# Low rotary keys on 128 partitions, and the probability scale on ScalarE, in a two-layer diffusion backbone

## The chip, the cores and the metric

One core of a Trainium2 chip runs the whole program. The metric is the device time of one launch in microseconds (us). Five engines work side by side, each through its own instructions in order: TensorE (PE; its weight loads are listed apart as PEld), VectorE (DVE), ScalarE (ACT), GpSimd (POOL) and SyncE (SP), which here issues DMAs. The granted TensorE clock is given as a share of 2.4 GHz.

## The reference, cut to what matters

Layer 0 is latent attention (8 heads, 512 latent queries against 256 context and 512 latent keys) and a squared-ReLU MLP; layer 1 is a gated MLP and another squared-ReLU MLP. The change touches the attention of layer 0 alone. There a key has 128 plain dimensions of its own head and 64 rotary dimensions that all heads share (`k_pe`), normed together:

```python
k_pe = jnp.broadcast_to(k_pe[:, :, None, :], (B, S, MLA_HEADS, QK_ROPE))
k = rmsnorm(jnp.concatenate([k_nope, k_pe], axis=-1), k_norm)
...
s = jnp.einsum('bqhd,bkhd->bhqk', qi, k, preferred_element_type=jnp.float32) * scale
p = jax.nn.softmax(s, axis=-1)
return jnp.einsum('bhqk,bkhd->bqhd', p.astype(v.dtype), v)
```

## The kernel before

Every fp32 operand of a matmul is split into a high part, rounded to the matmul's format, and a low part, the rest, and a product is the sum of high·high, high·low and low·high (`mm3`, lines 79 to 82). ACT makes the high part with a cast, DVE the low part by a subtraction (`split`, lines 70 to 77).

Attention (lines 604 to 717) goes through 16 steps, a head and a half of its queries each. The loop at line 703 writes down `scores` of the next step, then `values` of this one, and then filler work: projections of the next heads' keys, values and queries (`kv_proj`, `q_proj`), the output projection of finished heads (`out_proj`), and background steps that sum up the modulation weights on DVE (`ada_steps`, line 165). The last step's output projection is `out_last`. The order in which the engines get the instructions is not this one: a planner with a time model of its own (`schedule_with_timeline_sim`, line 982) sorts them by priority and expected readiness. The order on each engine is then fixed, and semaphores keep what depends apart.

`scores` (line 622) works on tiles of 128 queries by 768 keys, 32 of them in all. A tile takes ten matmuls of 384 columns: five pairs of operands, each over two halves of the keys (lines 630 to 633). The first three pairs are the plain dimensions. For the rotary dimensions the 64 high parts of a query and its 64 low parts lie one above the other on 128 partitions (`sq`, made at lines 311 to 319), and the high parts of the keys lie there twice (`rh`, line 536), so one pass gives (high + low)·high. The fifth pair is high·low: it takes the first 64 partitions of `sq` and the low parts of the keys, `rl`, a tile of 64 partitions (lines 216 and 537). Both come from one transposition of `kpe`, which holds the rotary keys twice side by side (line 530).

Then the softmax of the tile: a DVE instruction moves the scores out of PSUM, scaled, and takes their maximum (L637), DVE negates it (L639), ACT takes the exponential in place and its sum (L640), DVE takes the reciprocal of the sum (L641) and multiplies the 768 columns by it (L642). `values` transposes the result on PE (L655), ACT and DVE split it into `th` and `tl` (L72 and L73, from line 658), and PE multiplies with the values (L80 to L82 with output `o`). The score tile has one buffer in PSUM (`PS`), the probabilities `p` five in SBUF, the transposed ones `pt` three in PSUM.

Of the kernel before, what the change touches and what calls it, by code (L numbers as in the profile page):

```python
# [9 lines left out]
F32 = mybir.dt.float32  # L10
F32R = mybir.dt.float32r
BF16 = mybir.dt.bfloat16
AF = mybir.ActivationFunctionType
ALU = mybir.AluOpType
AX = mybir.AxisListType

P = 128
# [4 lines left out]
TOK = CTX + SEQ  # L22
# [4 lines left out]
ROPE = 64  # L27
# [19 lines left out]
def hybrid_dit_kernel(  # L47
# [7 lines left out]
    PE, ACT, DVE, POOL = nc.tensor, nc.scalar, nc.vector, nc.gpsimd  # L55
    SBUF, PSUM = bass.MemoryType.SB, bass.MemoryType.PSUM

    def pool(stack, name, bufs=1, space=SBUF, side="left"):
        return stack.enter_context(tc.tile_pool(name=name, bufs=bufs, space=space, side=side, reuse_waits="tile"))
# [150 lines left out]
    ap_ = pool(att, "att")  # L210
# [2 lines left out]
    cq_h = ap_.tile([P, 3, SEQ], F32R, name="cq_h")  # L213
    cq_l = ap_.tile([P, 3, SEQ], F32R, name="cq_l")
    rh = ap_.tile([P, TOK], F32R, name="rh")
    rl = ap_.tile([ROPE, TOK], F32R, name="rl")
    epk = ap_.tile([P, NT], F32, name="epk")
    cosT = ap_.tile([P, NT, ROPE], F32, name="cosT")
    sinT = ap_.tile([P, NT, ROPE], F32, name="sinT")
# [112 lines left out]
    with ExitStack() as ini_stack:  # L332
# [7 lines left out]
        def pt(name):  # L340
            return ps.tile([P, 512], F32, tag="t", bufs=2, name=name)

        def pa(name):
            return ps.tile([P, 512], F32, tag="a", bufs=6, name=name)
# [60 lines left out]
        with ExitStack() as xstack:  # L405
# [12 lines left out]
            for k in range(0, KT, 2):  # L418
                o = pa(f"xct{k}")
# [4 lines left out]
            for k in range(KT):  # L424
                o = pa(f"xt{k}")
# [7 lines left out]
        for t in range(NT):  # L433
            o = rp[0][:, t * P:(t + 1) * P] if t < 2 else rp[1][:, (t - 2) * P:(t - 1) * P]
# [18 lines left out]
        for k in range(KT):  # L453
# [6 lines left out]
            for t in range(NT):  # L460
                a_h, a_l = (ch, cl) if t < 2 else (hh[k], hl[k])
                s = bass.ts(t if t < 2 else t - 2, P)
# [23 lines left out]
        for t in range(NT):  # L486
# [8 lines left out]
            o = pt(f"ckt{t}")  # L495
            for j in range(2):
                PE.transpose(o[:, j * P:(j + 1) * P], ck[:, j * P:(j + 1) * P], ident)
            for j in range(2):
                s = slice(t * P, (t + 1) * P)
# [12 lines left out]
        for t in range(NL):  # L512
            o = pa(f"qa{t}")
            for k in range(KT):
                s = bass.ts(t, P)
# [15 lines left out]
        for u in range(2):  # L531
            o = pt(f"krt{u}")
            for j in range(3):
                PE.transpose(o[:, j * P:(j + 1) * P], kpe[:, 3 * u + j, :, :].rearrange("p a r -> p (a r)"), ident)
            s = slice(u * 384, (u + 1) * 384)
            ACT.copy(out=rh[:, s], in_=o[:, :384])
            DVE.tensor_tensor(out=rl[:, s], in0=o[:ROPE, :384], in1=rh[:ROPE, s].bitcast(F32), op=ALU.subtract)

        drain(kv0)

# [63 lines left out]
    with hst as st_:  # L604
# [17 lines left out]
        def scores(h, half):  # L622
            kh, kl, rk = Ks[h]
            rk = rk.rearrange("p (a b) -> p a b", a=2)
            qh, ql, sq, rq_ = Qs[h // 2]
            i = h % 2
            for t in (2 * half, 2 * half + 1):
                s = slice(t * P, (t + 1) * P)
                S = ps.tile([P, 2, 512], F32, tag="s", bufs=PS, name=f"s{h}{t}")
                ops = [(qh[:, i, s], kh), (qh[:, i, s], kl), (ql[:, i, s], kh), (sq[i][:, s], rh), (sq[i][:ROPE, s], rl)]  # L630
                for m, (a, b) in enumerate(ops):
                    for n in range(2):
                        PE.matmul(S[:, n, :384], lhsT=a, rhs=b[:, n * 384:(n + 1) * 384], start=m == 0, stop=m == 4)  # L633
                sm = hq.tile([P, 4], F32, tag="sm", bufs=4, name=f"sm{h}{t}")
                rq = rq_[:, t, i, 2:3]
                e = hq.tile([P, 2, 384], F32, tag="p", bufs=5, name=f"p{h}{t}")
                DVE.tensor_tensor_reduce(out=e, in0=S[:, :, :384], in1=rk, op0=ALU.mult, op1=ALU.max, scale=rq,  # L637
                                         scalar=-3.0e38, accum_out=sm[:, 0:1])
                DVE.tensor_scalar(out=sm[:, 1:2], in0=sm[:, 0:1], scalar1=-1.0, scalar2=None, op0=ALU.mult)  # L639
                ACT.activation(out=e, in_=e, func=AF.Exp, bias=sm[:, 1:2], accum_out=sm[:, 2:3])  # L640
                DVE.reciprocal(out=sm[:, 3:4], in_=sm[:, 2:3])  # L641
                DVE.tensor_scalar(out=e, in0=e, scalar1=sm[:, 3:4], scalar2=None, op0=ALU.mult)  # L642
                Pr[h, t] = e.rearrange("p a b -> p (a b)")

        def values(h, half):
# [45 lines left out]
        drain(q_proj(0)); ada_step(8)  # L691
        steps = [(h, half) for h in range(HEADS) for half in range(2)]
        scores(0, 0)
        drain(kv_proj(1))
        fill = {}
# [7 lines left out]
        for i, (h, half) in enumerate(steps):  # L703
            if i + 1 < len(steps):
                scores(*steps[i + 1])
            values(h, half)
            ada_step(ADS[i])
            for g, n in fill.get((h, half), []):
                drain(g, n)
            if i == len(steps) - 2:  # L710
                out_last(3, 0)
# [117 lines left out]
    with ExitStack() as st_:  # L829
# [7 lines left out]
        for q in range(4):  # L837
            ws = [W(gm_w_in, 2 * k2, 2, HALF + q * 512, 512, f"gv{q}{k2}") for k2 in range(4)]
            for ts in ((0, 1), (2, 3)) if q == 0 else ((0, 1, 2, 3),):
                acc = {t: (pu if t < 2 else pd)(f"v{q}{t}") for t in ts}  # L840
                for k in range(KT):
                    wh, wl = ws[k // 2]
                    for t in ts:
                        s = slice(t * P, (t + 1) * P)
                        mm3(acc[t], hs[k][0][:, s], hs[k][1][:, s], wh[:, k % 2, :], wl[:, k % 2, :], k == 0, k == KT - 1)
                for t in ts:
# [8 lines left out]
                            in_=gm_bs.rearrange("g p -> (g p)").unsqueeze(0).to_broadcast([P, G * P]))  # L855
        for g4 in range(2):
            o = pt(f"wst{g4}")
# [6 lines left out]
            o = pt(f"rsw{g4}")  # L864
# [33 lines left out]
        for t in range(NL):  # L898
# [3 lines left out]
                              op0=ALU.subtract, op1=ALU.mult)  # L902
# [83 lines left out]
```

## Time and profile before

| | |
|---|---|
| median of 3 runs | 1401.54 us (1399.29 to 1401.88) |
| the profiled execution | 1399.21 us |
| its span, from the first to the last instruction | 1397.4 us |
| busy: PE, DVE, ACT, POOL | 1355.4, 856.0, 545.6, 88.7 us |
| chain that ended last | PE 85%, issue 7%, DVE 3%, DMA 2%, ACT 1%, POOL 1% |
| granted TensorE clock, mean | 0.99 |

The profile is one execution. A busy share is an average over stages, and a PE that counts as busy may still stream fewer columns than it could, because a matmul's end is modelled. So a stage is read by the starts of neighbouring matmuls and by what its waits name.

### The profile page before, as it was taken

How to read it: one execution, taken by the hardware profiler on the slowest of the kernel's cores; microseconds unless marked ns; L12 is line 12 of the kernel's file. 1: busy time of each engine (PE TensorE's matmuls, PEld its weight loads, DVE VectorE, ACT ScalarE, POOL GpSimd, SP SyncE). 2: the span in 40 equal slices, each digit the busy share in tenths (PEclk: the TensorE clock that was granted, in tenths of full speed). 3: DMA queues.
4: the chain of work that ended last, by engine and by line, in shares of the span. 5: the costliest groups of instructions: out<-in, count | busy, mean ns of one | idle time of the engine just before them, and what ended most of it. 6: DMA issues, size and time to landing. Idle time of an engine off the chain costs nothing.

```text
span 1397.4 us, 18421 instructions
## 1 busy us (share of the span) xinstructions
PE 1355.4 (97%) x7159; PEld 1149.3 (82%) x7159; DVE 856.0 (61%) x1423; ACT 545.6 (39%) x1046; POOL 88.7 (6%) x140
## 2 busy tenths in 40 slices
PE   6989899999899999999999999999999999999998
PEld 4878889888898888888898888888888888888888
DVE  5876787887899888543457356555575344343442
ACT  6556556564652231322335233222254133231331
POOL 2031111100011111000000010000000000000000
PEclk9998999999999999999999999999999999999999
DMA  9551221311478878333323332222223222333311
GB/s 286 169 171 35 80 89 41 114 46 39 132 224 277 280 249 272 98 103 99 97 69 102 102 111 86 90 92 91 76 61 121 91 91 91 94 103 93 104 46 61
DMA packets 126823, 163.23 MB, mean 117 GB/s; under 512 B 7467, under 2 KB 111488, under 8 KB 126736
## 3 DMA queue, kind: packets, MB, share of 16 engines
q1 hardware_dynamic: 114784, 119.50, 27.0%
q0 software_dynamic: 11808, 42.03, 9.5%
q8 instruction: 56, 0.92, 0.3%
q10 hardware_dynamic: 144, 0.52, 0.1%
q14 instruction: 31, 0.25, 0.1%
HBM read 159.94 MB, written 2.10 MB: 116 GB/s over the span
## 4 chain that ended last, share of the span: by engine, by line
PE 85%; issue 7%; DVE 3%; DMA 2%; ACT 1%; POOL 1%; SPq 0%; POOLq 0%; DVEq 0%; ACTq 0%
PE s L633 3%; PE v L80 2%; PE v L82 2%; PE v L81 2%; DMA adr<-in_ada_w_dram 2%; PE pt L655 1%; PE wo L80 1%; PE f1d2o L82 1%; PE f1d0o L80 1%; PE f1d0o L81 1%; PE f1d2o L81 1%; PE f1d2o L80 1%; PE f1d0o L82 1%; PE f0d1o L80 1%; PE f0d1o L81 1%
## 5 line engine op out<-in xcount | busy, mean ns | idle before, releaser
L165 DVE SCALAR_TENSOR_TENSOR acc<-adr,sil,acc 128x1024 f32<-128x1024 f32 x70 | 89.7, 1281 | 20.7 <-DMA adr<-in_ada_w_dram 20.0
L161 POOL DMA_DIRECT2D adr<-in_ada_w_dram x80 | 43.4, 542 | 220.9 <-DVE acc L165 122.6
L782 DVE TENSOR_TENSOR f1a<-f1a 128x512 f32<-128x512 f32 (+1 forms) x36 | 22.5, 629 | 39.8 <-ACT f1a L781 39.8
L637 DVE CUSTOM_DVE_ANT_0 p<-s,rk,rq 128x768 f32<-128x768 f32 x32 | 32.5, 1015 | 14.1 <-PE s L633 11.9
L73 DVE TENSOR_TENSOR tl<-pt,th 128x512 fp32r<-128x512 f32 x48 | 32.7, 687 | 11.6 <-ACT th L72 11.2
L72 ACT CAST f0uh<-f0a 128x512 fp32r<-128x512 f32 (+1 forms) x36 | 20.4, 572 | 48.5 <-DVE f0a L782 48.5
L72 ACT CAST th<-pt 128x512 fp32r<-128x512 f32 x48 | 27.9, 589 | 23.6 <-PE o L82 13.6
L640 ACT ACTIVATE p<-p,sm 128x768 f32<-128x768 f32 x32 | 30.1, 940 | 15.1 <-DVE sm L639 15.1
L126 POOL TENSOR_TENSOR nst<-nst,mhalf 128x2 f32<-128x2 f32 x6 | 5.1, 854 | 457.5 <-DVE nst L125 457.5
L73 DVE TENSOR_TENSOR f1ul<-f1a,f1uh 128x512 fp32r<-128x512 f32 (+1 forms) x36 | 22.6, 632 | 18.8 <-ACT f1uh L72 18.6
L782 DVE TENSOR_TENSOR f0a<-f0a 128x512 f32<-128x512 f32 (+1 forms) x36 | 22.5, 627 | 18.4 <-ACT f0a L781 18.4
L72 ACT CAST f1uh<-f1a 128x512 fp32r<-128x512 f32 (+1 forms) x36 | 20.4, 572 | 32.0 <-DVE f1a L782 32.0
L73 DVE TENSOR_TENSOR f0ul<-f0a,f0uh 128x512 fp32r<-128x512 f32 (+1 forms) x36 | 22.4, 627 | 11.7 <-ACT f0uh L72 11.7
L81 PE MATMUL o<-tl,vh 128*128 128x256 f32 x96 | 28.1, 292 | 1.0 <-DVE tl L73 0.9
L80 PE MATMUL o<-th,vh 128*128 128x256 f32 x96 | 28.6, 298 | 0.0
L600 DVE SCALAR_TENSOR_TENSOR xT<-wo,mod,xT 128x512 f32<-128x512 f32 (+1 forms) x40 | 25.1, 638 | 5.2 <-PE wo L82 4.9
L655 PE MATMUL pt<-ident,p 128*128 128x128 f32 x192 | 27.7, 274 | 0.0
L82 PE MATMUL o<-th,vl 128*128 128x256 f32 x96 | 27.1, 282 | 0.0
L655 PEld LDWEIGHTS pt<-ident,p 128*128 128x128 f32 x192 | 22.2, 141 | 1.8 <-issue 1.0
L892 DVE TENSOR_TENSOR gm<-gm,u 128x512 f32<-128x512 f32 x16 | 11.0, 689 | 20.6 <-ACT u L873 20.5
L81 PEld LDWEIGHTS o<-tl,vh 128*128 128x128 f32 x96 | 18.2, 190 | 2.4 <-DVE tl L73 1.7
L642 DVE TENSOR_SCALAR p<-p,sm 128x768 f32<-128x768 f32 x32 | 19.8, 618 | 0.6
(2637 smaller groups left out, 4651.6 us busy)
## 6 DMA issues: line engine op xcount, KB each, us to landing
adr<-in_ada_w_dram POOLq DMA_DIRECT2D x80, 512.0 KB, 4.8
xn<-in_x_dram SPq DMA_DIRECT2D x4, 512.0 KB, 7.2
out_dram<-of SPq DMA_DIRECT2D x8, 256.0 KB, 2.2
xn<-in_ctx_dram SPq DMA_DIRECT2D x2, 512.0 KB, 4.1
ada000r<-in_ada_w_dram SPq DMA_DIRECT2D x1, 512.0 KB
ada001r<-in_ada_w_dram SPq DMA_DIRECT2D x1, 512.0 KB
ada100r<-in_ada_w_dram SPq DMA_DIRECT2D x1, 512.0 KB, 11.3
ada101r<-in_ada_w_dram SPq DMA_DIRECT2D x1, 512.0 KB, 10.2
```

What stands on the lines that cost most here:

```text
L72: ACT.copy(out=hi, in_=src)
L73: eng.tensor_tensor(out=lo, in0=src, in1=hi.bitcast(F32), op=ALU.subtract)
L80: PE.matmul(o, lhsT=wh, rhs=mh, start=start, stop=False)
L81: PE.matmul(o, lhsT=wh, rhs=ml, start=False, stop=False)
L82: return PE.matmul(o, lhsT=wl, rhs=mh, start=False, stop=stop)
L161: nc.gpsimd.dma_start(out=r, in_=ada_w[l][k * P:(k + 1) * P, ch * D:(ch + 1) * D])
L165: DVE.scalar_tensor_tensor(out=acc, in0=r, scalar=sil[:, k, 0:1], in1=acc, op0=ALU.mult, op1=ALU.add)
L633: PE.matmul(S[:, n, :384], lhsT=a, rhs=b[:, n * 384:(n + 1) * 384], start=m == 0, stop=m == 4)
L637: DVE.tensor_tensor_reduce(out=e, in0=S[:, :, :384], in1=rk, op0=ALU.mult, op1=ALU.max, scale=rq, scalar=-3.0e38, accum_out=sm[:, 0:1])
L640: ACT.activation(out=e, in_=e, func=AF.Exp, bias=sm[:, 1:2], accum_out=sm[:, 2:3])
L655: PE.transpose(T[:, j, q * P:(q + 1) * P], Pr[h, 2 * half + q][:, (2 * jp + j) * P:(2 * jp + j + 1) * P], ident)
L782: DVE.tensor_tensor(out=f, in0=f, in1=f, op=ALU.mult)
```

## The change

`rl` gets 128 partitions in place of 64 and is filled on all of them (the transposition already holds the keys twice, so the lower half is the same numbers again). The fifth pair of matmuls then takes all 128 partitions of `sq`: it adds low·low, which was left out before, to high·low. The number of matmuls and their columns stay. And the multiplication by the reciprocal of the sum, a DVE instruction, becomes an ACT instruction that copies in place with a scale of one number per partition.

```diff
-    rl = ap_.tile([ROPE, TOK], F32R, name="rl")
+    rl = ap_.tile([P, TOK], F32R, name="rl")
...
-            DVE.tensor_tensor(out=rl[:, s], in0=o[:ROPE, :384], in1=rh[:ROPE, s].bitcast(F32), op=ALU.subtract)
+            DVE.tensor_tensor(out=rl[:, s], in0=o[:, :384], in1=rh[:, s].bitcast(F32), op=ALU.subtract)
...
-                ops = [(qh[:, i, s], kh), (qh[:, i, s], kl), (ql[:, i, s], kh), (sq[i][:, s], rh), (sq[i][:ROPE, s], rl)]
+                ops = [(qh[:, i, s], kh), (qh[:, i, s], kl), (ql[:, i, s], kh), (sq[i][:, s], rh), (sq[i][:, s], rl)]
...
-                DVE.tensor_scalar(out=e, in0=e, scalar1=sm[:, 3:4], scalar2=None, op0=ALU.mult)
+                ACT.activation(out=e, in_=e, func=AF.Copy, scale=sm[:, 3:4])
```

## Rows read from the trace of the kernel before

**Rows 1.** Busy time by stage: us, engines' busy time (instructions), clock, DMA

```profile
119.00:352.00 233.00, 228.86 (x1493) 204.65 (x1491) 183.11 (x424) 137.14 (x393) 25.99 (x28) 0.99 0.21 66
352.00:385.00 33.00, 28.33 (x201) 26.61 (x201) 30.08 (x67) 20.69 (x42) 3.51 (x5) 0.90 0.46 146
```

**Rows 2.** Who waited for whom on PE, 119 to 352 us: total, times, longest

```profile
PE rkb L276 <- POOL st L271: 1.9, 1, 1.9
PE s L633 <- ACT qh L72: 1.4, 1, 1.4
PE o L81 <- DVE tl L73: 0.9, 2, 0.7
```

**Rows 3.** The score matmuls' line, L633: durations in ns (min/median/max), shapes, idle

```profile
L633 PE MATMUL s<-rh,sq x64: 332/338/340, 124.5 to 347.6; 128*128 128x384 f32 x64
L633 PEld LDWEIGHTS s<-rl,sq x64: 182/184/187, 124.9 to 347.9; 64*128 64x128 f32 x64
L633 PE MATMUL s<-rl,sq x64: 327/385/441, 124.9 to 348.1; 64*128 64x384 f32 x64
...
  issue: 7.8, 32
```

**Rows 4.** Timeline of PE and PEld, one score tile: start, us, engine, line

```profile
186.80 0.51 PE L633 MATMUL s<-kh,ql 128*128 128x384 f32 x2
187.15 0.51 PE L633 MATMUL s<-rh,sq 128*128 128x384 f32 x2
187.59 0.61 PE L633 MATMUL s<-rl,sq 64*128 64x384 f32 x2
188.13 0.38 PE L80 MATMUL o<-th,vh 128*128 128x256 f32 x1
188.36 0.28 PE L81 MATMUL o<-tl,vh 128*128 128x256 f32 x1
188.47 0.28 PE L82 MATMUL o<-th,vl 128*128 128x256 f32 x1
...
186.98 0.36 PEld L633 LDWEIGHTS s<-rh,sq 128*128 128x128 f32 x2
187.59 0.29 PEld L633 LDWEIGHTS s<-rl,sq 64*128 64x128 f32 x2 [0.25 <-issue]
188.13 0.19 PEld L80 LDWEIGHTS o<-th,vh 128*128 128x128 f32 x1 [0.25 <-issue]
```

**Rows 5.** Timeline of PE and PEld where weights of 4 rows follow

```profile
28.87 0.28 PE L389 MATMUL ada_o<-ada101l,c 128*4 128x256 f32 x1
...
28.75 0.09 PEld L389 LDWEIGHTS ada_o<-ada101l,c 128*4 128x4 f32 x1
29.08 0.52 PEld L394 LDWEIGHTS ada_c<-sel,adrow 4*128 4x128 f32 x4 [0.24 <-issue]
```

**Rows 6.** Lines L642, L640, and of ACT by shape (busy us, mean ns)

```profile
L642 DVE TENSOR_SCALAR p<-p,sm x32: 606/619/622, 131.1 to 351.6; 128x768 f32<-128x768 f32 x32
L640 ACT ACTIVATE p<-p,sm x32: 923/939/961, 129.0 to 350.4; 128x768 f32<-128x768 f32 x32
L640 ACT ACTIVATION_READ_ACCUMULATOR p<-p,sm x32: 182/190/222, 129.8 to 351.2; 128x1 f32 x32
...
L75 ACT ACTIVATE kh<-kt,gqk 128x512 fp32r<-128x512 f32 x7 | 4.9, 703 | 0.6 <-PE kt L265 0.6
```

**Rows 7.** Timeline of DVE, ACT and PE, the tile with the longest softmax

```profile
282.65 0.16 DVE L641 RECIPROCAL sm<-sm 128x1 f32<-128x1 f32 x1
284.96 0.61 DVE L642 TENSOR_SCALAR p<-p,sm 128x768 f32<-128x768 f32 x1
...
279.77 0.21 ACT L640 ACTIVATION_READ_ACCUMULATOR p<-p,sm 128x1 f32 x1
280.62 0.59 ACT L72 CAST th<-pt 128x512 fp32r<-128x512 f32 x1 [0.35 <-PE o L82]
...
282.65 0.36 PE L80 MATMUL o<-th,vh 128*128 128x256 f32 x1
...
289.38 0.60 PE L655 MATMUL pt<-ident,p 128*128 128x128 f32 x4
```

**Rows 8.** Timeline of ACT, DVE, PEld and PE, the last tile

```profile
351.31 1.06 ACT L72 CAST th<-pt 128x512 fp32r<-128x512 f32 x2
351.64 0.62 DVE L642 TENSOR_SCALAR p<-p,sm 128x768 f32<-128x768 f32 x1
352.91 0.19 PEld L81 LDWEIGHTS o<-tl,vh 128*128 128x128 f32 x1 [0.31 <-DVE tl L73]
354.75 1.04 PE L655 MATMUL pt<-ident,p 128*128 128x128 f32 x8
```

**Rows 9.** Busy time in a stretch of attention at a lower clock (columns of rows 1)

```profile
258.00:260.60 2.60, 2.60 (x8) 2.10 (x7) 1.82 (x5) 0.81 (x4) 0.98 (x2) 0.51 0.17 30
```

## Prediction

> **What bounds the kernel now.** The page comes first: PE is busy 97% of the span and takes 85% of the chain that ended last, so the question in each stage is whether PE streams as fast as it can. The change sits in attention, so I cut the span by stages. Attention runs from 119 to 352 us: PE is busy for 228.9 of its 233 us, DVE for 183.1 (79%) and ACT for 137.1 (59%) [rows 1]. In the next stage, to 385 us, DVE is busy for 30.1 of 33 us and PE for 28.3 [rows 1]; there PE is no longer alone at the bound. The waits of PE in attention name only 4.2 us: one of 1.9 us for POOL, one of 1.4 us for ACT, two for DVE [rows 2]. So neither ACT nor DVE holds PE up in attention, and a gain there has to come out of PE's own stream.
>
> Busy hides what that stream loses. The score matmuls' line shows it: of ten matmuls of a tile, those with `rl` alone use 64 rows. Their median duration is 385 ns against 338 for the same columns on 128 rows, and before the 64-row loads the load unit stands for 7.8 us in 32 times, with no wait named: 0.24 us once per tile [rows 3]. The timeline of one tile shows both ends. Pairs of 384 columns follow each other at 0.35 us (186.80 to 187.15). The 64-row pair starts 0.44 us after the pair before it, the next matmul 0.54 us after that, and the one behind, after only 256 columns, 0.23 us later, where the next takes 0.11 [rows 4]. The loads explain it: a 128-row load runs while the matmul before it streams (186.98, ahead of the pair at 187.15), but the first 64-row load starts when the last 128-row matmul has nearly ended (187.15 + 0.51 = 187.66 against 187.59), and the first 128-row load after it again starts late, at 188.13. Both have 0.25 us of idle load unit in front [rows 4]. Another place with few rows looks alike: a 4-row load waits 0.24 us, until the 128-row matmul that began at 28.87 and took 0.28 has nearly ended (29.15 against 29.08) [rows 5]. So it goes with the change in the number of rows, not with `rl` or its data.
>
> **The change part by part.**
>
> *128 rows in the fifth pair.* The ten matmuls keep their columns; what goes is the two switches. In an even stream the matmul at 188.36 would come 0.35 + 0.35 + 0.12 = 0.82 us after 187.15; it came after 1.21 [rows 4]. The excess is 0.39 us, and 32 tiles make 12.5 us, all in PE's queue. The added low·low product costs nothing in columns: the 128-row pair beside it is the price, 0.35 us a pair [rows 4]. Bounds: if only the entry's idle (7.8 us in all [rows 3]) went and the return stayed, 7.8; if both go, 12.5. I take 12.5, since the pairs ahead of the fifth are of exactly the form that it takes on.
>
> The TensorE page of the Trainium skill (TensorE: Matmul & The Clock Gate, section on packing small matmuls) says that a weight load overlaps a running matmul only when their row groups differ. By that rule 128 rows everywhere would be the bad case. The trace disagrees: the `rh` loads run under matmuls on the same 128 rows, and the loads that wait are those whose rows differ [rows 4].
>
> *The fill of `rl`* is done on 128 partitions in place of 64, twice, before the scores begin: the columns are the same, as is the partition's share of SBUF. I cost it at nothing; the cover is that the same instruction already runs there.
>
> *The multiplication leaves DVE:* 32 × 0.619 = 19.8 us [rows 6], off an engine for which PE waits 0.9 us in this stage [rows 2]. On the path that is worth between 0 and that 0.9; I take 0.
>
> *The copy on ACT.* The trace has no copy of 768 columns with a scale per partition. The nearest rows are the exponential over the same 768 columns, SBUF to SBUF with a number per partition, at 0.939 us, and the scaled copy of 512 columns out of PSUM, at 0.703 [rows 6]. I take 0.94, from the same shape: 32 × 0.94 = 30.1 us. ACT's load in attention becomes (137.1 + 30.1) / (233 − 12.5) = 76%, DVE's (183.1 − 19.8) / 220.5 = 74%. Neither becomes the bound by its sum.
>
> The ScalarE page (ScalarE: Activation LUTs, rules for kernel authors) tells authors to keep multiplications on VectorE, not ScalarE. The durations agree with it, 0.62 us against about 0.94, but that is a matter of engine time, not of the path. Its formula for a pointer operand gives 0.92 us as an estimate.
>
> *The new wait.* The copy sits in ACT's queue and waits for the reciprocal, on DVE. Behind it on ACT queue the `th` casts, the `kn`, `vh` and `kh` evacuations and the next exponential; PE waits for the casts. If ACT reaches the copy at once after its exponential, it stands for the reciprocal (0.16 us) and two hand-overs, some 0.24 us as an estimate from the 0.16, and then works 0.94: 1.18 us for what is behind. In the tile with the longest softmax the sum was out at 279.98 (279.77 + 0.21), and the reciprocal came only at 282.65, behind other DVE work: an ACT queue stuck there would have lost 2.7 us. In that time ACT cast a `th` (280.62 to 281.21) that PE first read at 282.65, 1.4 us later [rows 7]. So a copy of 0.94 in front of a cast is covered in a typical place, 1.18 just so, 2.7 not. The planner decides which it is; since it knows the wait, I expect it to put the ready casts first, as it put them here before the scale.
>
> *The probabilities come later* by 0.94 − 0.62 = 0.32 us and by the queue. In the tight tile the scale ended at 285.57 and the transposition came at 289.38, 3.8 us later [rows 7]; in the last tile it ended at 352.26 and the transposition came at 354.75, 2.5 us later [rows 8]. Both cover it.
>
> *The tail.* At 351.31 ACT casts two `th`, and PE waits 0.31 us for their low halves [rows 8]. If the last copy is put ahead of those casts, PE loses the 1.18 us; if behind, nothing. I take half, 0.6.
>
> *Order and clock.* The planner gets other durations and may sort the stage anew. PE's clock was at 0.51, the level of 1.2 GHz, in the 2.6 us from 258.0, after single-column matmuls of the background; a stretch like it costs 1.3 us [rows 9]. One more or one fewer is ±1.3; I take 0.
>
> *Sum*, on the profiled execution (1399.2 us, its span 1397.4 and 1.8 around it): 1399.2 − 12.5 + 0.6 = 1387.3. After 352 us everything is released by what comes before it, so the gain is kept. The median of the runs lies 2.3 us above the profiled one; I put the forecast in the middle, 1388.5.
>
> **The rivals.**
>
> *ACT gets late and PE waits for it: slower.* The mechanism is the copy in front of `th` casts, with ACT standing for the reciprocal. The gain is gone when a tile costs PE over 0.39 us. For it speaks that PE leans on ACT at every `th`, 48 times, and that the copy can stand for up to 2.7 us [rows 7]; against it, that PE waited for ACT just once in 233 us [rows 2]. If half of the 1.18 us of each tile reaches PE, it costs 32 × 0.59 = 18.9 us: 1399.2 − 12.5 + 18.9 = 1405.6.
>
> *ACT takes back a part.* A quarter of the 1.18 us reaches PE: 32 × 0.3 = 9.4, so 1396.
>
> *The switch stays.* The change would not do what it says, if the idle belonged to `rl` as a second operand and not to its rows: 1399.2 to 1401.5. The 4-row loads speak against it [rows 5].
>
> *The page's rule on row groups holds.* Then each of the three loads at and after the fifth pair would wait for the matmul in front, at about 0.2 us each, 0.6 in place of 0.39: 32 × 0.2 = 6.4 us more, 1405.6. The running overlap at 186.98 speaks against it [rows 4].
>
> **How the numbers follow.** The forecast has 0.75; ACT taking back a part 0.12; the switch staying 0.05; ACT making it slower 0.07; the rule 0.01. A measurement of this kernel can tell about 0.2%, 2.8 us, from no change. So faster is 0.75 + 0.12 = 0.87, within 0.2% is 0.05, slower 0.08. The range: downward, the 4.2 us of waits [rows 2] and the clock's 1.3 us [rows 9] could go too: 1387.3 − 5.5 = 1381.8, so 1382. Upward it takes in the part taken back, 1396, with a little of the runs' spread: 1397.
>
> **What would show it.** In the profile after: 128-row loads for `rl` with no idle of 0.24 us before them and pairs at 0.35 us; a score matmul median of 338 ns in all five pairs; attention shorter by 12 us, to some 221; copies on ACT of about 0.94 us, 32 times; PE's waits for ACT in attention still a few us. I would be wrong if PE's waits for `th` and `tl` grow to over 10 us, if the 0.25 us stay before the `rl` loads, or if the next stage, to 385 us, grows by what attention gives.

## The result, and the profile after

| | before | after |
|---|---|---|
| median of 4 runs | 1401.71 us | 1390.88 us (1389.81 to 1392.8) |
| ratio, 95% interval | | 0.993 [0.9917, 0.9942] |
| the profiled execution, its span | 1399.21, 1397.4 us | 1390.98, 1389.2 us |
| busy: PE, DVE, ACT | 1355.4, 856.0, 545.6 us | 1346.8, 838.6, 569.6 us |

The kernel is faster by 0.7%, 10.8 us between the medians. The forecast was 1388.5 us; the measured time lies 2.4 us above it and inside the range.

The line of the score matmuls in the profile after, durations in ns (min/median/max), answers [rows 3]:

```profile
L633 PE MATMUL s<-kh,qh x64: 333/338/445, 121.0 to 342.3; 128*128 128x384 f32 x64
L633 PE MATMUL s<-rh,sq x64: 333/337/422, 126.0 to 343.4; 128*128 128x384 f32 x64
L633 PEld LDWEIGHTS s<-rl,sq x64: 187/188/193, 126.2 to 343.5; 128*128 128x128 f32 x64
L633 PE MATMUL s<-rl,sq x64: 334/338/423, 126.4 to 343.7; 128*128 128x384 f32 x64
...
  issue: 0.5, 1
```

The fifth pair now takes as long as the others, 338 ns in the median where it took 385, and of the 32 idle times of 7.8 us one of 0.5 is left. The timeline of PE and PEld in the tile that [rows 4] showed:

```profile
186.57 0.51 PE L633 MATMUL s<-kh,ql 128*128 128x384 f32 x2
186.92 0.51 PE L633 MATMUL s<-rh,sq 128*128 128x384 f32 x2
187.26 0.51 PE L633 MATMUL s<-rl,sq 128*128 128x384 f32 x2
187.61 0.60 PE L655 MATMUL pt<-ident,p 128*128 128x128 f32 x4
...
187.09 0.36 PEld L633 LDWEIGHTS s<-rl,sq 128*128 128x128 f32 x2
187.44 0.31 PEld L655 LDWEIGHTS pt<-ident,p 128*128 128x128 f32 x2
```

The pairs follow each other at 0.34 to 0.35 us through the fifth and into the next matmul, and the loads for `rl` (187.09) run while the `rh` pair (186.92 to 187.43) streams.

The stages, in the columns of [rows 1]; attention now ends earlier, so the first stretch takes in a few us of what follows:

```profile
119.00:352.00 233.00, 228.11 (x1561) 217.42 (x1560) 172.92 (x411) 166.88 (x436) 27.11 (x29) 0.99 0.21 66
```

In the same 233 us PE gets 1561 matmuls done in place of 1493. ACT is busy for 166.9 us in place of 137.1. The copies themselves, and what ACT waits for in front of them (the line of L642, durations in ns; then, from ACT's waits from 121 to 346.6 us, the one ahead of L642: total, times, longest):

```profile
L642 ACT ACTIVATE p<-p,sm x32: 929/942/1018, 131.4 to 346.7; 128x768 f32<-128x768 f32 x32
...
ACT p L642 <- DVE sm L641: 3.4, 6, 1.6
```

PE's waits in attention (121 to 354 us, columns of [rows 2], the three longest) stay small: 0.6 us for the low halves `tl`, far from the 10 us that the prediction named as a sign of being wrong.

```profile
PE q L80 <- DVE qg L304: 1.8, 1, 1.8
PE s L633 <- ACT qh L72: 0.8, 1, 0.8
PE o L81 <- DVE tl L73: 0.6, 2, 0.3
```

To see where the time went I take attention from the first score matmul's start (the `kh,qh` row of L633) to the last value matmul's start (the last of L82 with output `o`). Before, that is 119.5 to 361.6, 242.1 us; after, 121.0 to 353.8, 232.8 us: 9.3 us less, where the prediction's sign was 12. Up to the first score matmul the profiled execution of after lost 1.5 us, with the same instructions in the same order but for the shape of `rl`'s fill; among the runs below whose instructions are the same up to there, that start lies between 119.4 and 125.0 us. And `rl` itself is filled 1.3 us later already (107.9 us against 106.6), so the delay is older than the changed instruction and belongs to the execution. Behind attention the gain is kept: the last span differs by 8.2 us = 9.3 − 1.5 + 0.4.

### The profile page after: what moved, and what is told of

Its sections match the earlier page's. It is cut to its first block, busy times and chain, and to the rows that moved or that the text cites. A ratio compares the mean times of both kernels' runs of the same rounds, so it can differ in the third digit from the quotient of the medians.

```text
span 1389.2 us, 18418 instructions
## 1 busy us (share of the span) xinstructions
PE 1346.8 (97%) x7159; PEld 1153.9 (83%) x7159; DVE 838.6 (60%) x1391; ACT 569.6 (41%) x1078; POOL 89.1 (6%) x140
## 4 chain that ended last, share of the span: by engine, by line
PE 77%; issue 9%; DVE 6%; DMA 5%; ACT 2%; POOL 1%; SPq 0%; POOLq 0%; DVEq 0%; ACTq 0%
DMA adr<-in_ada_w_dram 5%; PE s L633 3%; PE v L82 2%; PE v L80 2%; PE v L81 2%; DVE acc L165 1%; PE pt L655 1%; PE f1d2o L80 1%; PE f1d0o L81 1%; PE f1d0o L82 1%; PE f1d0o L80 1%; PE f1d2o L81 1%; PE f1d2o L82 1%; PE f1d1o L80 1%; PE f0d2o L82 1%
## 5 line engine op out<-in xcount | busy, mean ns | idle before, releaser
L640 ACT ACTIVATE p<-p,sm 128x768 f32<-128x768 f32 x32 | 30.2, 943 | 12.6 <-DVE sm L639 12.5
L642 ACT ACTIVATE p<-p,sm 128x768 f32<-128x768 f32 x32 | 30.4, 950 | 3.4 <-DVE sm L641 3.4
L82 PE MATMUL o<-th,vl 128*128 128x256 f32 x96 | 27.1, 283 | 0.0
L633 PE MATMUL s<-kh,qh 128*128 128x384 f32 x64 | 18.3, 363 | 1.6 <-ACT qh L72 0.8
```

What stands on the lines that cost most here:

```text
L82: return PE.matmul(o, lhsT=wl, rhs=mh, start=False, stop=stop)
L642: ACT.activation(out=e, in_=e, func=AF.Copy, scale=sm[:, 3:4])
```

## The experiments

Theory A: the gain is the two changes of the row count in each score tile, and ScalarE's copy gives a small part back. The rivals are B (the copy is free; the planner's new order eats the rest), C (the freed VectorE is the gain), D (the cost goes with the 64-row matmuls, not with the change), and those that came up on the way.

The order of the instructions shows how clean each experiment is. With the rows alone, every engine has the order of before. With the copy alone, every engine has the order of after. So the four make a square: two orders, each with 64 and with 128 rows. The order comes with the copy, and the rows leave it alone.

In every table row, attention is measured as above. Beside it stands how long the granted clock was at 0.50, the level of 1.2 GHz, in that time, and from where on. In the profile after one such stretch lies at 163.4; its window (columns of [rows 1]):

```profile
163.40:166.80 3.40, 3.40 (x16) 3.40 (x16) 2.26 (x7) 1.32 (x5) 1.58 (x2) 0.50 0.57 165
```

Those come and go between executions of one kernel: the 128 rows alone had none in one profile and one in the next, and so had the whole change.

| kernel | ratio to before, 95% interval | attention, us | at half clock, us (from) |
|---|---|---|---|
| before | 1 | 242.1 | 3.4 (257.1) |
| after | 0.993 [0.9917, 0.9942] | 232.8 | 3.4 (163.4) |
| after, again | 0.9927 [0.9914, 0.9941] | 232.7 | 0 |
| 128 rows alone | 0.9922 [0.9901, 0.9942] | 230.4 | 0 |
| 128 rows alone, again | 0.9918 [0.9903, 0.9933] | 230.0 | 3.4 (165.5) |
| copy alone | 1.0006 [0.9992, 1.0019] | 245.9 | 6.8 (175.0, 260.3) |
| four changes of rows | 1.0083 [1.0061, 1.0106] | 253.2 | 0 |
| copy twice | 0.9986 [0.9974, 0.9999] | 238.8 | 10.2 (162.3, 176.0) |
| 96 rows | 0.9926 [0.9908, 0.9943] | 230.4 | 3.4 (161.5) |
| 72 rows | 0.992 [0.9901, 0.9938] | 231.1 | 3.4 (167.4) |
| 32 rows | 0.9999 [0.9986, 1.0011] | 240.6 | 0 |
| 128 rows, sums on VectorE | 0.9967 [0.9955, 0.998] | 228.5 | 0 |

What such a stretch costs can be read where two executions run the same matmuls in the same order. Those inside a stretch of 3.4 us take 1.5 to 1.6 us longer in every such pair. But part of it can come back. PE in the 128 rows alone, without a stretch and then with the one from 165.5 us:

```profile
169.84 0.51 PE L633 MATMUL s<-kl,qh 128*128 128x384 f32 x2
171.18 0.39 PE L81 MATMUL o<-tl,vh 128*128 128x256 f32 x1 [0.82 <-DVE tl L73]
```

```profile
174.87 0.51 PE L633 MATMUL s<-kl,qh 128*128 128x384 f32 x2
175.22 0.29 PE L81 MATMUL o<-tl,vh 128*128 128x256 f32 x1
```

The wait for `tl` that follows is gone in the second; I read that as the engines that feed PE drawing level while it was slow. So the two profiles differ by 0.4 us in attention (230.4 and 230.0), not by 1.6, and those of the whole change by 0.1 (232.7 and 232.8). The stretch of before, at 257.1, cost nearly all of its price: 32 rows, in the same order and without one, take 1.5 us less. So I compare profiles without a stretch where there are any. Where there are none I take off the price inside: 1.6 us for before (240.5) and, as an estimate that nothing came back, 3.1 for the copy alone (242.8).

### The rows alone

The change's three edits of `rl`; the scale stays `DVE.tensor_scalar`.

> The low rotary keys on 128 partitions alone; the scale by the reciprocal stays on VectorE. Theory A (the row switch was worth 0.39 us a tile, 12.5 us in all, and ScalarE's copy gave some 3 us of it back): ratio to the kernel before near 0.991, some 2 to 3 us faster than the whole change; the time from the first score matmul to the last value matmul falls from 242.1 us to about 230, and PE's excess over an even stream there, apart from the switches, stays at the 7.4 us of before. Rival B (the copy costs nothing, the gain is simply smaller because the planner sorted attention anew): the same ratio as the whole change, 0.993, and an excess of about 10 us here too.

Ratio 0.9922, attention 230.4 us. That is the gain of the whole change and, by the profiles, some 2 us more. Since PE's order is that of before, the two traces can be laid side by side, matmul by matmul: the steps at the fifth pair and right behind it are shorter by 11.5 us in all, 0.36 us a tile, and everything else by 0.2: the 1.6 us of half clock are gone, and 1.4 us came in as slightly longer steps elsewhere, 0.5 of it within the first pair of the score matmuls. What lengthens them the profile does not name. Theory A's sign holds. What it calls the excess did not stay: against an even stream, in which each matmul takes the median step of its number of columns (222.3 us in all), 8.1 us are left over here, and no half clock is in them as in the 7.4.

### The copy alone

The last edit of the change alone; `rl` and the fifth pair stay as before.

> The scale on ScalarE alone; the fifth pair of score matmuls keeps its 64 rows. Theory A: slower than before by 0 to 4 us (ratio 1.000 to 1.003), the 0.25 us of idle load unit ahead of the 64-row loads still there 32 times, and the excess over an even stream some 3 us up. Rival B: no change of time beyond 1 us in either direction, apart from what another order brings. Rival C (freed VectorE time is what gained, the rows nothing): 8 to 10 us faster.

Ratio 1.0006, with 1 inside the interval: moving VectorE's 19.8 us to ScalarE gains nothing, so rival C falls. (The same edit adds the copy to ScalarE, so it does not show what freeing VectorE would do by itself.) Attention is 245.9 us; without its two stretches at half clock some 242.8, against 240.5, so 2.3 us more. The waits of PE in attention, before in [rows 2], now:

```profile
PE o L81 <- DVE tl L73: 2.4, 3, 1.1
PE q L80 <- DVE qg L304: 1.8, 1, 1.8
PE s L633 <- ACT qh L72: 0.6, 1, 0.6
PE wo L80 <- DVE qg L304: 0.4, 1, 0.4
```

In all they name 5.2 us against 4.2. The wait for the low halves of the transposed probabilities, `tl`, went from 0.9 to 2.4 us. They are made from ACT's casts, which is the place that the prediction named for lateness.

### Four changes of the row count in place of two

```diff
-                for m, (a, b) in enumerate(ops):
-                    for n in range(2):
-                        PE.matmul(S[:, n, :384], ...)
+                for m, n in [(0, 0), (0, 1), (1, 0), (1, 1), (2, 0), (2, 1), (3, 0), (4, 0), (3, 1), (4, 1)]:
+                    a, b = ops[m]
+                    PE.matmul(S[:, n, :384], ...)
```

> The kernel before, with the last four score matmuls of a tile in the order 128 rows, 64 rows, 128 rows, 64 rows in place of two and two: the same ten matmuls, but four changes of the number of rows a tile in place of two. Theory A (the cost goes with the change of rows): slower by 32 x 0.39 = 12.5 us, ratio 1.009. Rival D (the cost goes with the 64-row matmuls or with the tile of the low keys, however they are ordered): no change, ratio 1.000.

Slower by 0.83% [0.61, 1.06], some 11.6 us; attention 253.2 us, 12.7 more than before without its half clock, where A said 12.5 and D nothing. The load unit's timeline in one tile:

```profile
192.06 0.19 PEld L633 LDWEIGHTS s<-rh,sq 128*128 128x128 f32 x1
192.50 0.18 PEld L633 LDWEIGHTS s<-rl,sq 64*128 64x128 f32 x1 [0.25 <-issue]
192.87 0.19 PEld L633 LDWEIGHTS s<-rh,sq 128*128 128x128 f32 x1 [0.18 <-issue]
193.24 0.18 PEld L633 LDWEIGHTS s<-rl,sq 64*128 64x128 f32 x1 [0.19 <-issue]
193.60 0.19 PEld L80 LDWEIGHTS o<-th,vh 128*128 128x128 f32 x1 [0.18 <-ACT p L640]
```

Each change of rows, in both directions, has its idle in front, and the loads that would run under a matmul in an even stream come 0.37 us apart where the matmuls need 0.17. The edit also puts two matmuls in a row on the same half of the score tile; that is not the cause, since the matmuls into `o` do the same at 0.11 us [rows 4]. The cost goes with the change; D falls.

### The copy twice

The whole change with `ACT.activation(out=e, in_=e, func=AF.Copy)` behind the first copy.

> The whole change with a second copy in place on ScalarE behind the first, so 30 us more on that engine (89% of attention) and 0.94 us more before the probabilities are ready. Theory A (PE pays for part of each copy through late casts, some 0.1 us each so far): the second costs more than the first, 5 to 15 us, ratio to before 0.997 to 1.004. Rival B (the copy lies beside PE's work and costs nothing): within 2 us of the whole change, ratio 0.993.

Ratio 0.9986, about 0.0058, 8 us, above the whole change. So the copies do not lie beside PE's work for nothing, and the second costs more than the first. In the profile attention is 238.8 us against 232.7 and 232.8, with 10.2 us at half clock against 0 and 3.4. The window from 160 to 200 us shows it, here and in the second profile of the whole change:

```profile
160.00:200.00 40.00, 36.25 (x223) 33.71 (x223) 31.31 (x71) 28.38 (x76) 7.90 (x11) 0.87 0.42 127
```

```profile
160.00:200.00 40.00, 35.30 (x236) 32.74 (x237) 31.86 (x73) 26.69 (x73) 8.92 (x11) 1.00 0.44 134
```

PE idles for about as long in both (3.8 and 4.7 us of 40), but the clock is at 0.87 in the first. One profile cannot say whether that is chance, but the runs say more: over the whole program the granted clock was 0.9868 in the mean of the 12 executions with two copies (0.984 to 0.989) and 0.9888 in that of the 10 of the whole change (0.987 to 0.991). That is 2.8 us of 1400, as an estimate, if PE loses all of it, so up to a third of the 8 us is clock. The waits that the profile names in attention sum to 6.7 us against 5.7 and 4.6; the rest has no name. PE's order is another here too, so the cost is that of the copy with its order.

### The rows and the whole change on one chip

> Once more the 128 rows alone, now on the same chip as the whole change. Theory A (ScalarE's copy costs PE little once the clock's dips, which come and go from one execution to the next, are set aside): ratio 0.992, attention 230 to 231 us from the first score matmul to the last value matmul without dips. It is 0.5 to 2 us faster than the whole change, less than the rounds can tell. Rival E (the copy costs some 3 us of the 12.5): 3 us faster than the whole change.

> The whole change again, on the same chip as the 128 rows alone. Theory A: ratio 0.992 to 0.994, attention 231 us after subtracting 1.7 us for each dip of the clock. Rival E: ratio 0.994 to 0.995.

0.9918 against 0.9927: 1.3 us, less than either interval. By the profiles without a stretch the whole change's attention is 232.7 us, that of the rows alone 230.4; by those with one it is 232.8 against 230.0, 230.4 and 231.1 (128, 96 and 72 rows, in the mean 230.5). So the copy costs PE 2.3 us in attention with 128 rows, and by the estimate above 2.3 with 64. By names, PE's waits in the second profile of the whole change sum to 5.7 us, in the first of the rows alone to 4.1 (1.9 + 1.4 + 0.8):

```profile
PE o L81 <- DVE tl L73: 1.9, 3, 0.9
PE q L80 <- DVE qg L304: 1.8, 1, 1.8
PE s L633 <- DVE sm L637: 0.6, 2, 0.4
PE s L633 <- ACT qh L72: 0.6, 1, 0.6
PE qrt L316 <- DVE qs L73: 0.4, 1, 0.4
PE wo L80 <- DVE qg L304: 0.4, 1, 0.4
```

That names 1.6 us of it, 1.1 for `tl`. Rival E's 3 us and A's 0.5 to 2 both lie within what the runs leave open; whether the copy or the order that comes with it is to blame cannot be told apart, since the planner makes the order from the copy.

### 96, 72 and 32 rows

From the rows alone, with `sq[i][:96, s]`, `sq[i][:72, s]` and `sq[i][:32, s]` in the fifth pair and `rl` cut alike. Every engine keeps its order.

> The 128-row version with the scale on VectorE, but the fifth pair of score matmuls takes 96 of its 128 rows (so a part of low times low is left out); every engine's order is that of the 128 rows alone. Theory A (any change of the number of rows costs the drain on both sides, 0.36 us a tile): slower than the 128 rows alone by 11.5 us, ratio to before near 1.000, 0.25 us of idle ahead of the 96-row loads. Rival F (the cost goes with the share of rows left out, or with half arrays alone): between 0.992 and 0.996.

> As the 96-row version, with 72 rows in the fifth pair of score matmuls. Theory G (what costs is a change between more than 64 rows and 64 or fewer; 72 rows count as a full array): like the 128 rows, ratio 0.992, no idle of 0.25 us ahead of the loads. Theory H (the cost depends on how far the rows fall below 128, and 96 was near enough): between 0.994 and 1.000.

> 32 rows in the fifth pair, so half of high times low is left out as well. Theory G: the same drain on both sides as with 64 rows, 11 to 12.5 us more than with 128 rows, ratio to before 0.999 to 1.001. Theory H: more than the 64 rows cost, ratio above 1.002. If only exactly half an array has the drain: 0.992.

With 96 rows theory A failed: ratio 0.9926, as with 128. Going from 128 rows to 96 and back costs nothing. That made theory G, that 64 rows or fewer are one case and more are another, and the last two runs bore it out: 72 rows 0.992, 32 rows 0.9999. Where between 64 and 72 the boundary lies, no run shows. The loads for `rl` in the three (busy us, mean ns, then the idle time before them):

```profile
L633 PEld LDWEIGHTS s<-rl,sq 96*128 96x128 f32 x64 | 11.6, 189 | 0.0
```

```profile
L633 PEld LDWEIGHTS s<-rl,sq 72*128 72x128 f32 x64 | 11.6, 189 | 0.0
```

```profile
L633 PEld LDWEIGHTS s<-rl,sq 32*128 32x128 f32 x64 | 9.4, 183 | 7.8 <-issue 7.8
```

With 32 rows the idle is 7.8 us in all, to the tenth what 64 rows had [rows 3], and attention takes 240.6 us against 240.5. The return to 128 rows costs the same idle again:

```profile
188.48 0.29 PEld L633 LDWEIGHTS s<-rl,sq 32*128 32x128 f32 x2 [0.25 <-issue]
189.02 0.19 PEld L80 LDWEIGHTS o<-th,vh 128*128 128x128 f32 x1 [0.25 <-issue]
```

So neither does the price grow as the rows get fewer: H falls too.

### The background sums on VectorE

The rows alone, and in `ada_steps` the three sums that fall in attention take the path of the later ones (`fast`): no single-column matmuls.

> The 128 rows alone, and the three background sums that fall in attention no longer use 48 single-column matmuls but the way of the later sums: a transposition and a reduction on VectorE and one matmul each. If PE's bursts of single-column matmuls cost their own time and bring the dips of the clock behind them: 3 x 1.7 us less on PE and up to 1.7 us for a dip that does not come, so 3 to 6 us faster than the 128 rows alone, ratio to before 0.988 to 0.990, and no dip between the first score matmul and the last value matmul. If VectorE's 3 x 2.5 us more, or the planner's other order, weigh as much: ratio 0.992 or above.

Ratio 0.9967, 7 us slower than the rows alone. The longest wait of PE in its profile stands ahead of attention, with two of the new DVE instructions shortly before its end (the line numbers are one higher in this kernel):

```profile
PE krt L535 <- DVE kpe L531: 7.6, 1, 7.6
...
102.47 1.23 DVE L174 STREAM_TRANSPOSE adr02t<-acc 128x1024 f32<-128x1024 f32 x1
105.71 1.21 DVE L175 TENSOR_REDUCE red<-adr02t 128x32 f32<-128x1024 f32 x1
```

The planner put the first sum among the rotation of the keys, for which PE waits, and the first score matmul came at 129.1 us. The two instructions are 2.4 of the 7.6 us; the rest goes with the other order. Attention then took 228.5 us with the single-column matmuls gone, 1.9 less than the rows alone without half clock (230.4). That is less than the 3 to 6 forecast, and less than what was lost ahead of it. No half clock appeared in attention, but neither did it in some kernels that kept the single-column matmuls, so this says nothing on what brings it.

## Why the prediction was right, and where not

**PE's stream bounds attention: right.** Moving 19.8 us from VectorE to ScalarE, where it takes 30.1, gained nothing and cost some 2 us by the profiles, and what left PE's queue came off the time.

**The switch, 12.5 us: the right mechanism, the term a fifth too large.** The stretch around the fifth pair is shorter by 0.34 to 0.39 us in 31 of the 32 tiles, 11.5 us in all, so 0.39 was the upper end and not the mean. And some of what PE gained there it lost again: 1.2 to 1.4 us in longer steps elsewhere in the stage, for which the step "I take 12.5" had no term. What is left is 10.2 us, from 240.6 (32 rows) to 230.4 (128 rows), both without half clock; the ratios of the kernels with 72, 96 and 128 rows and the scale on VectorE give 10.4 to 11.5. The copy's order gives the same, 242.8 − 232.7 = 10.1; doubling the switches cost 12.7.

**"It goes with the change in the number of rows": too wide.** The two rows of evidence were 64 and 4 [rows 3, 5]. Both lie on the same side of what the runs found: 72 and 96 rows join 128 without idle. For the change that made no difference, but it was argued from two cases as if from all.

**The rule on row groups.** The TensorE page of the Trainium skill (TensorE: Matmul & The Clock Gate, section on packing small matmuls) says that a weight load overlaps a running matmul only when their row groups differ. The trace disagrees after as before: `rl`'s 128-row loads run under matmuls on the same rows, 187.09 against 186.92 to 187.43.

**The copy, 0.94 us: right** (0.942 in the median). **Its cost, 0.6 us in the tail: too small and in the wrong place.** It cost 2.3 us in attention by the profiles without half clock, and 0.8 to 1.3 by the ratios, whose intervals also allow nothing. Of the 2.3, 1.1 is the larger wait for `tl` (1.9 against 0.8 us). The tail was covered: the next stage ends as much earlier as attention does. The break-even of 0.39 us a tile was never near: 2.3 / 32 = 0.07. Standing for the reciprocal took ACT 3.4 us in 6 times, as expected from a planner that puts ready work first.

**The order, "I take 0":** the copy did sort attention anew on PE, and the rows did not. What that order costs by itself stays open. **The clock, ±1.3 us:** the window of [rows 9] begins 0.9 us into the stretch. A whole one, 257.1 to 260.5, is 1.6 us, it differs between executions of one kernel, and where a wait follows most of it can come back. **The fill of `rl`:** 558 ns in place of 550, twice: nothing, as said.

**The sum.** From the profiled execution, 1399.2 − 10.2 (the rows) + 2.3 (the copy) − 1.4 (the half clock, 1.5 us net before and 0.1 after) + 1.5 (the start, the execution's own) − 0.4 (behind attention) = 1391.0, as measured; each term is a difference between profiles, so the sum has to close. Against it the forecast's 1387.3 has 2.3 us too much for the rows and 1.7 too little for the copy, both in the same direction. That the start and the clock nearly cancel is luck.

**The better version.** The rows without the copy have the better ratio in both comparisons (0.9922 and 0.9918 against 0.993 and 0.9927) and by the profiles some 2 us in attention, but the intervals overlap: some 0.1% better, if at all.

## What to carry to other kernels

Where PE bounds a stage, look at the starts of neighbouring matmuls and at the idle of the load unit with no wait named: a matmul over few rows in the middle of full ones (64 or 32 here, not 72 or 96) can cost more than the columns that it streams. Operands that already lie twice on the partitions can fill the rows for nothing. And moving work from an engine for which PE hardly waits to one that feeds PE bought nothing here: it cost some 2 us, and a second copy 8 more.

## What the runs showed of the hardware that was not expected

- A weight load of 72 or 96 rows followed and preceded by 128-row matmuls had no idle (0.0 us in 64 loads); with 64 and with 32 rows it had 7.8 us, 0.24 for each pair, and the return to 128 rows the like (0.25 us ahead of the first load).
- The same pair of 384 columns takes 0.35 us of PE's stream on 72, 96 and 128 rows, and the 32-row pair costs as much as the 64-row one: fewer rows saved nothing anywhere.
- With the same instructions up to there, the first score matmul started between 119.4 and 125.0 us, and stretches at half clock were there in some executions and not in others. The matmuls inside one of 3.4 us took 1.5 to 1.6 us longer, but in the rows alone the wait of 0.8 us behind it was gone, and attention came out no longer (230.0 against 230.4 us). To subtract the whole price from a profile can take off too much.
